# A diffusion trunk step on one core: first queries, unit copies, weight parts and memory masks take other places in the order of the work

## The chip, the cores and the metric

The kernel runs on one core of a Trainium2 chip. The metric is the time of one execution on the device, in microseconds (us); lower is better. Of several executions the median is given. A core has five engines that run side by side: PE (matmul; PEld is its weight load), DVE (vector), ACT (scalar and activation functions), POOL and SP; here SP and POOL issue the transfers between the chip's main memory and the core (DMA). Each engine works through its own queue in order; an instruction that must wait for another engine or a transfer holds up all that stand behind it in its queue.

## The reference

One layer of a trunk with 128 context tokens and 512 latent tokens (640 in all), width 1024: a gated feed-forward half step, a token mixer of two branches side by side, and a second half step. The two branches are what matters here:

```python
# differential attention, 8 heads, for a block of 128 queries
s = einsum('bqhcd,bkhcd->bhcqk', q, k) * scale          # two score maps (c = 0, 1)
pr = softmax(s)
w = pr[:, :, 0] - lam * pr[:, :, 1]
out = einsum('bhqk,bkhv->bqhv', w, v)
# mLSTM memory, 4 heads, two directions, over chunks of 128 tokens
b = cumsum(log_f); log_d = where(tril, b_t - b_s + i_s, -inf)
m_t = maximum(b + m, max(log_d)); dmat = exp(log_d - m_t)
s = (q k^T) * dmat
num = s v + exp(b + m - m_t) * (q C);  den = the same with n in place of C
h = num / maximum(abs(den), exp(-m_t))
C_new = decay * C + sum(w_s k_s v_s)
...
hm = rmsnorm(h_f + reverse(h_b)) * sigmoid(mo)
y = sigmoid(gm) * (hm @ w_br_m) + sigmoid(gd) * (att @ w_br_d)
```

Before the attention, queries and keys are normalised, and those of the latent tokens are rotated by their position (rope).

## The kernel before

All matmuls use float32 values in two parts: a high part that PE takes (`wH`, `hH`, `kH`, ...), made by a copy on ACT, and a low part (`wL`, `hL`, `kL`), the rest that remains, made by a subtraction on DVE. A product is then three matmuls (high x high, low x high, high x low). Helpers carry the lines that the profile shows: L51 is any ACT operation (`act`), L54 a DVE operation on two tensors (`tt`), L57 one with a scalar besides (`stt`), L61 one with a scalar alone (`ts`), L75 a matmul, L78 a transpose on PE. A scheduler places each engine's instructions; `written()` keeps what stands under it in the order of the code, and `issue_after(x)` keeps what stands under it behind instruction x.

**Projection units.** While the attention runs, a queue `fill` computes further projections in the gaps. `fill.units(n)` runs n units, each of 24 matmuls into a PSUM buffer `ps_t` (or `ps_p`), and a copy from it on ACT into `k_tok`, `q_tok`, `v_tok` or `stage`. `fill.ahead()` makes the high part `wH` of the next weights on ACT (128x2048, from the buffer `raw` that SP loads); `fill.low()` makes `wL` on DVE.

**Gate rows and the first head.** `gate_rows` turns the memory's gates into rows of numbers, step by step (`next(rows)`); its results are `fg`, `e`, `b`, `MP`, `dc`, `ig` on DVE, and ACT's exponentials of them, called `Q`. Around it stand head 0's keys (`kH`, `kL`), its queries (`queries()`, L1677: `qT` by a copy on ACT, then its low part by DVE at L54) and the first scores.

**Turns of the attention.** For each of 8 heads there are 5 turns of 128 queries: `scores` (PE, into `sc`), `soft` (DVE `mn`, ACT exponentials `p`, DVE `rc`, `r`, `p`), `mix` (PE transposes `ps_wT`, ACT copies `wT`), `values` of the turn before (PE, into `ps_o`). `aside` lets a step of the rotation (`rotate()`: `rope`, `rt`, `ry`, `qkt`, `qky`) run beside it. A table UNITS says how many units each turn has in its first and second part; n[1] is the second.

**The memory.** For each of 4 heads `load()` fetches `P` (rows of gate numbers, from `nm_dram`) and the values `va`, and adds the masks to both halves of `P` on DVE; `prep(i)` (i = 0 to 4) takes exponentials of `P` on ACT and multiplies by q k^T from `ps_st`. Then ten cells follow, numbered n = 0 to 9, each `cell()` with `ps_n` and `ps_u` on PE, `num` on ACT and DVE, `C` (the update) on DVE and `den` ending in a reciprocal (`at_vec`). A list `later[n]` holds what is issued behind cell n: the next head's `prep` behind cells 3 to 7, the last head's `finish` (`hs`, times `ry` and `g_mh`) behind cells 4 to 8. L814 is a DVE operation that computes modulation columns (`columns.tile`), placed between cells.

Of the kernel before, what the change touches and what calls it, by code (L numbers as in the profile page):

```python
# [7 lines left out]
F32 = mybir.dt.float32  # L8
# [3 lines left out]
ALU = mybir.AluOpType  # L12
# [19 lines left out]
def tile_trunk(ctx: ExitStack, tc: tile.TileContext, a: dict):  # L32
    nc = tc.nc
    vec = nc.vector
    as_written = [False]

    def placed(ins):
        if as_written[0] is in_row:
            i = ins.ins
            if i.engine in in_row:  # L40
                tc.add_manual_dep(
                    i, in_row[i.engine].name, mybir.DependencyInfo(mybir.DependencyClass.NoSync, mybir.DependencyReason.DATA),
                    reason="written",
                )
            in_row[i.engine] = i
        elif as_written[0]:
            tc.keep_in_program_order(ins)
        return ins

    def act(*args, **kw):  # L50
        return placed(nc.scalar.activation(*args, **kw))  # L51

    def tt(eng, out, in0, in1, op):
        return placed(eng.tensor_tensor(out=out, in0=in0, in1=in1, op=op))  # L54
# [13 lines left out]
    @contextmanager  # L68
    def written():
        was, as_written[0] = as_written[0], in_row  # L70
        yield
        as_written[0] = was
# [1335 lines left out]
    fill = Fill()  # L1408
# [94 lines left out]
    def gate_cols(j):  # L1503
        Q = Q_at[j]
        for i0, n in ((0, 4), (4, 1)):
            p = psum.tile([128, 4, 128], F32, tag="mm", name="ps_c")
            for i in range(n):
                tr(p[:, i, :], Q[:, (i0 + i) * 128 : (i0 + i + 1) * 128], ident)
            vec.tensor_copy(
                cols[:, i0 : i0 + n, 2 * j : 2 * j + 2, :].rearrange("p i q (d h) -> p i (q d) h", d=2),  # L1510
                p[:, :n].rearrange("p i (b c) -> p i b c", c=32)[:, :, :, 0:4],
            )
# [63 lines left out]
    def rotate():  # L1576

        if not rotations:
            return False
        first, second = rotations[0], rotations[1] if len(rotations) > 1 else []  # L1580
        had, left = len(first), len(second)
        with written():
            if had == 4 and left == 7 or had == 2 and left == 5:
                second.pop(0)()
            else:
                first.pop(0)()
                if (had, left) in ((5, 8), (4, 6)):
                    second.pop(0)()
            if not first:
                rotations.pop(0)  # L1590
        return True
# [53 lines left out]
    class Head:  # L1645
# [32 lines left out]
        def queries(self):  # L1678
            self.qT = ap.tile([128, 2, T], F32R, tag="qT", name="qT")
            self.ao = ap.tile([128, 5, 128], F32, tag="ao", name="ao")  # L1680
            self.at_q = act(self.qT, self.qd, AF.Copy)
            r = slice(64, 128)
            tt(vec, self.qT[r], self.qd[r], self.qT[r].bitcast(F32), ALU.subtract)

        def keys(self, *parts):
            if 0 in parts:
# [284 lines left out]
    heads = [Head(hd) for hd in range(8)]  # L1971
# [87 lines left out]
    rows = gate_rows(gt, ps_g)  # L2059
# [6 lines left out]
    with tc.issue_after(heads[0].at_copy.ins):  # L2066
        heads[0].keys(0, 1, 2)
    fill.units(1)
    next(rows)
    fill.units(2)  # L2070
    heads[0].queries()
    for _ in rows:
        pass
    fill.units(2)
# [2 lines left out]
    def aside(hd, qi, part):  # L2077
        if part == 0:
            with written():
                split = fill.low()  # L2080
            if qi < 4 and (UNITS[hd][qi][1] or not split):
                rotate()
        elif qi != 3:
            rotate()
        if (hd, part) == (0, 1) and qi < 2:
            gate_cols(qi)
# [6 lines left out]
    for hd in range(8):  # L2093
        H = heads[hd]
        odd = hd % 2
        N = heads[hd + 1] if hd < 7 else None
        for qi in range(5):
            n = UNITS[hd][qi]
            with written():
                H.scores(qi)  # L2100
                if qi > 0:
                    H.turn(qi - 1)
                if late is not None and qi == 2:
                    late()
                    late = None
                H.soft(qi)
            aside(hd, qi, 0)
            fill.units(n[0])
            with written():
                H.mix(qi)  # L2110
            if 0 < qi < 4 or hd == 7 and qi:
                with written():
                    H.values(qi - 1)
            if qi in (2, 3) and hd < 7:
                with written():
                    (N.turn_keys, N.turn_queries)[qi - 2]()
            if qi == 3 and hd < 7:
                N.load_cache()
            aside(hd, qi, 1)
            if (hd, qi) == (0, 2):  # L2120
                begin_pools()
            elif (hd, qi) == (6, 2):
                begin_memory()
            fill.units(n[1])
            if n[1]:
                rotate()
            with written():
                fill.ahead()
        n = UNITS[hd][-1]
        if hd < 7:  # L2130
            with written():
                fill.units(n[0])
                H.values(3)
                H.turn(4)
                N.keys(0)
                N.queries()
                N.keys(1, 2)
                fill.units(n[1])
                H.values(4)
            H.finish_norm()  # L2140
            with written():
                fill.ahead()
            fill.units(n[2])
            late = H.finish
        else:
            with written():
                H.turn(4)
            fill.eager = True
            fill.units(1)
            H.values(4)  # L2150
            H.finish_norm()
            fill.drain(3)
            with written():
                H.finish()
# [9 lines left out]
    mask = load(mp, [128, 2, 128], a["mask"], name="mask")  # L2164

    fill.pace(0.8, 1)
    class Memory:
# [6 lines left out]
        def load(self, fetch=nc.sync.dma_start):  # L2174
            h = self.h
            self.P = mp.tile([128, 5, 2, 128], F32, tag="P", name="P", bufs=2)
            self.va = mp.tile([128, 5, 258], F32, tag="va", name="va", bufs=2)
            for d in range(2):
                fetch(
                    out=self.P[:, :, d, :], in_=nm_dram[32 * d + h].partition_broadcast(128).rearrange("p (c t) -> p c t", c=5)  # L2180
                )
            fetch(out=self.va[:, :, 0:256], in_=v_dram[h])
            vec.memset(self.va[:, :, 256:257], 1.0)
            vec.memset(self.va[:, :, 257:258], 0.0)
            with ExitStack() as st:
              if h == 1:
                st.enter_context(tc.issue_after(mem[0].at_P.ins))
              for d in range(2):
                tt(vec, self.P[:, :, d, :], self.P[:, :, d, :], mask[:, d, None, :].to_broadcast([128, 5, 128]), ALU.add)
            self.ktok = mp.tile([128, 5, 256], F32, tag="ktok", name="mktok", bufs=2)  # L2190
            self.hs = mp.tile([128, 5, 256], F32, tag="hs", name="hs", bufs=2)

        def load_c(self):
            self.C = [load(mp, [128, 2, 258], a["c_aug"][d, self.h], tag=f"C{d}", name="C", bufs=2) for d in range(2)]
# [113 lines left out]
    mem = [Memory(h) for h in range(4)]  # L2308
    in_order[0] = True
    mem[0].load(dma)  # L2310
    mem[0].load_c()
    csil2 = ada_p.tile([128, 2, D], F32, name="csil")
    dma(csil2, csil_dram.partition_broadcast(128))
# [11 lines left out]
    for h in range(4):  # L2325
        m = mem[h]
        later = [[] for _ in range(10)]
        if h < 3:
            mem[h + 1].load()
            for i in range(5):  # L2330
                later[3 + i].append(lambda i=i: mem[h + 1].prep(i))
        if h > 0:
            for i in range(5):
                later[4 + i].append(lambda i=i: mem[h - 1].finish(i))
        if h == 3:
            for k in range(KT):
                later[2 + k].append(attended)
        later[9].append(m.gate)
        steps = [(s, 0, s >= 2, True, s < 3) if d == 0 else (3 - s, 1, s >= 2, True, s < 3) for s in range(4) for d in range(2)]
        steps += [(4, d, d == 1, False, True) for d in range(2)]  # L2340
        for n, (st, then) in enumerate(zip(steps, later)):
            if st[0] == 4 and st[1] == 0 and h < 3:
                mem[h + 1].load_c()
            m.cell(*st)
            if n in ((5,), (3, 7), (3, 7), ())[h]:
                columns.tile(m.at_vec)
            for f in then:
                f()
            fill.slot(0)
        m.stats()  # L2350
# [113 lines left out]
    for i in range(2):  # L2464
        r = raw[:, i * 1024 : (i + 1) * 1024]
# [7 lines left out]
    st = [Stats(x, hf, tmp) for hf in range(2)]  # L2473
# [224 lines left out]
```

## Time and profile before

| | us |
|---|---|
| median of 3 runs | 1796.81 |
| lowest and highest of them | 1793.94, 1798.72 |
| the profiled execution | 1796.18 |
| its span, from the first to the last instruction | 1794.3 |
| PE busy | 1767.4 (99%) |
| DVE busy | 1338.4 (75%) |
| ACT busy | 892.0 (50%) |

The span is the time between the first and the last instruction of the profiled execution; 1.88 us lie around it. A row of the timeline gives an instruction's start and duration in us, engine, line, operation, output<-inputs, shapes and a count; in brackets stand the engine's idle time before it and what ended that idle time.

### The profile page before, as it was taken

To read this page: it belongs to the slowest core of one execution; us is meant where nothing else is said; L and a number is where in the kernel's file an instruction comes from. 1 tells how busy PE (TensorE), PEld (TensorE's weight loads), DVE (VectorE), ACT (ScalarE), POOL (GpSimd) and SP (SyncE) were. 2 spreads that over 40 slices of the span, in tenths; PEclk is the share of its full clock that TensorE was granted. 3 is DMA by queue.
4 is the path that set the end of the run, shared out by engine and by line. 5 is a ranking of instruction groups with operands and counts; after the bars stand their busy time and mean duration, and the time that the engine had idled before them with its cause. 6 is when DMAs were issued, how large, how long until landed. Compare 5 with 4: busy or idle time off the path is not lost.

```text
span 1794.3 us, 29420 instructions
## 1 busy us (share of the span) xinstructions
PE 1767.4 (99%) x11790; PEld 1700.2 (95%) x11790; DVE 1338.4 (75%) x2136; ACT 892.0 (50%) x1563; POOL 40.8 (2%) x72
## 2 busy tenths in 40 slices
PE   8999999999999999999999999999999999999998
PEld 7999999999999999888889998899999999999998
DVE  5979897577889868776765637876768888896475
ACT  5554544332655555565655446562327545544432
POOL 0000000101000000000000000000000000000010
PEclk9999999999999999999999999999999999999999
DMA  8354565978235563333333345565642446557992
GB/s 321 121 200 159 197 243 197 368 224 279 92 109 197 180 188 88 107 105 102 105 119 126 126 157 167 205 235 200 219 165 77 152 160 197 205 176 276 354 311 84
DMA packets 149468, 327.03 MB, mean 182 GB/s; under 512 B 11537, under 2 KB 107537, under 8 KB 137553
## 3 DMA queue, kind: packets, MB, share of 16 engines
q1 hardware_dynamic: 137954, 279.38, 46.0%
q0 software_dynamic: 10688, 43.13, 7.4%
q10 hardware_dynamic: 688, 2.63, 0.4%
q8 instruction: 93, 1.52, 0.3%
q14 instruction: 45, 0.37, 0.1%
HBM read 243.12 MB, written 71.49 MB: 175 GB/s over the span
## 4 chain that ended last, share of the span: by engine, by line
PE 82%; DVE 8%; DMA 6%; ACT 3%; issue 1%; SPq 0%; DVEq 0%; ACTq 0%
PE ps_f L75 49%; PE ps_p L75 15%; PE ps_t L75 8%; PE sc L75 2%; PE ps_o L75 2%; DVE ww L54 2%; PE ps_n L75 1%; DMA P<-nm_dram 1%; DMA raw_a<-in_w_ada_k 1%; PE ps_wT L78 1%; DMA raw<-in_w2b 1%; DVE junk L814 1%; PE ps_u L75 1%; DMA a_raw<-aT_dram 1%; DVE wL L54 1%
## 5 line engine op out<-in xcount | busy, mean ns | idle before, releaser
L75 PE MATMUL ps_f<-S,ww 128*128 128x320 f32 x2400 | 387.0, 309 | 3.0 <-DMA S<-g_dram 1.0
L75 PEld LDWEIGHTS ps_f<-S,ww 128*128 128x128 f32 x2400 | 359.8, 188 | 7.0 <-DVE ww L54 4.6
L54 DVE TENSOR_TENSOR ww<-raw,ww 128x2048 fp32r<-128x2048 f32 (+1 forms) x73 | 163.9, 2245 | 65.3 <-ACT ww L51 65.2
L75 PE MATMUL ps_f<-hm,ww 128*128 128x320 f32 x1176 | 185.6, 309 | 0.1
L75 PEld LDWEIGHTS ps_f<-hm,ww 128*128 128x128 f32 x1176 | 175.7, 188 | 0.3 <-DVE ww L54 0.3
L51 ACT ACTIVATE ww<-raw 128x2048 fp32r<-128x2048 f32 (+1 forms) x73 | 136.8, 1874 | 56.6 <-DVE raw L54 32.8
L54 DVE TENSOR_TENSOR raw<-raw 128x1024 f32<-128x1024 f32 x186 | 160.9, 865 | 2.4
L75 PE MATMUL ps_f<-hm,wB 128*128 128x320 f32 x1008 | 161.5, 309 | 0.0
L75 PE MATMUL ps_p<-hH,wH 128*128 128x320 f32 x480 | 150.7, 314 | 2.1 <-DVE num L54 2.1
L75 PE MATMUL ps_t<-wH,hH 128*128 128x256 f32 (+1 forms) x440 | 150.8, 343 | 2.0 <-DVE x L57 0.9
L75 PEld LDWEIGHTS ps_f<-hm,wB 128*128 128x128 f32 x1008 | 151.3, 188 | 0.0
L75 PE MATMUL ps_p<-hH,wL 128*128 128x320 f32 x480 | 148.3, 309 | 0.0
L75 PE MATMUL ps_p<-hL,wH 128*128 128x320 f32 x480 | 148.3, 309 | 0.0
L75 PE MATMUL ps_t<-wH,hL 128*128 128x256 f32 (+1 forms) x440 | 146.4, 333 | 0.9 <-DVE hL L54 0.9
L75 PE MATMUL ps_t<-wL,hH 128*128 128x256 f32 (+1 forms) x440 | 146.2, 332 | 0.0
L51 ACT ACTIVATE u<-ps_f 128x320 f32<-128x320 f32 x129 | 55.7, 432 | 158.1 <-PE ps_f L75 157.9
L54 DVE TENSOR_TENSOR wL<-raw,wH 128x2048 fp32r<-128x2048 f32 x37 | 84.6, 2286 | 23.9 <-ACT wH L51 23.9
L51 ACT ACTIVATE wH<-raw 128x2048 fp32r<-128x2048 f32 (+1 forms) x45 | 75.4, 1681 | 48.4 <-PE ps_p L75 38.5
L54 DVE TENSOR_TENSOR wB<-raw,wB 128x1024 fp32r<-128x1024 f32 x64 | 78.1, 1220 | 24.1 <-ACT wB L51 24.1
L814 DVE CUSTOM_DVE_ANT_0 junk<-raw_a,csil 128x1024 bf16<-128x1024 f32 (+1 forms) x76 | 92.6, 1218 | 3.3 <-DMA raw_a<-in_w_ada_c 3.0
L75 PEld LDWEIGHTS ps_t<-wH,hH 128*128 128x128 f32 x440 | 83.8, 190 | 10.1 <-ACT nsq L51 1.1
L75 PEld LDWEIGHTS ps_p<-hH,wH 128*128 128x128 f32 x480 | 90.2, 188 | 3.0 <-DVE num L54 2.5
(305 smaller groups left out, 3526.2 us busy)
## 6 DMA issues: line engine op xcount, KB each, us to landing
g_dram<-g SPq DMA_DIRECT2D x44, 640.0 KB, 7.6
raw_a<-in_w_ada_c POOLq DMA_DIRECT2D x38, 512.0 KB, 5.1
g_dram<-g SPq DMA_DIRECT2D x24, 480.0 KB, 8.3
raw<-in_w1b SPq DMA_DIRECT2D x11, 1024.0 KB, 4.9
raw<-in_w3b SPq DMA_DIRECT2D x11, 1024.0 KB, 6.2
raw<-in_w1a SPq DMA_DIRECT2D x10, 1024.0 KB, 5.0
raw<-in_w3a SPq DMA_DIRECT2D x10, 1024.0 KB, 6.3
qk_d<-qk_t SPq DMA_DIRECT2D x64, 160.0 KB, 2.9
```

Source lines behind the costliest of these rows:

```text
L51: return placed(nc.scalar.activation(*args, **kw))
L54: return placed(eng.tensor_tensor(out=out, in0=in0, in1=in1, op=op))
L75: tc.keep_in_program_order(nc.tensor.matmul(*args, **kw))
L78: tc.keep_in_program_order(nc.tensor.transpose(*args, **kw))
L814: placed(vec.tensor_tensor_reduce(out=junk, in0=raw, in1=self.csil[:, v, :], op0=ALU.mult, op1=ALU.add, scale=1.0, scalar=0.0, accum_out=m ...
```

## The change

It has three parts. No arithmetic and no tile size is altered; PE's instructions stay as they are, in the same order.

1. Head 0's `queries()` are called ahead of the last two steps of `gate_rows`; the second of these is held behind the low part of `qT`.
2. In a turn, `fill.ahead()` moves. Where the turn's second part has units, it comes right behind them, in written order, and ahead of the further rotation step; where it has none, it comes ahead of the rotation step of `aside`.
3. The mask additions leave `load()` and become a function of their own, `masked()`. For head 0 it is called right behind the load, for heads 1 to 3 behind cell n = 2 of the head before, and held behind that cell's reciprocal.

```diff
-            tt(vec, self.qT[r], self.qd[r], self.qT[r].bitcast(F32), ALU.subtract)
+            self.at_low = tt(vec, self.qT[r], self.qd[r], self.qT[r].bitcast(F32), ALU.subtract)
...
     fill.units(1)
+    heads[0].queries()
     next(rows)
     fill.units(2)
-    heads[0].queries()
+    with tc.issue_after(heads[0].at_low.ins):
+        next(rows, None)
     for _ in rows:
         pass
...
+            if not n[1]:
+                with written():
+                    fill.ahead()
             aside(hd, qi, 1)
...
-            fill.units(n[1])
             if n[1]:
+                with written():
+                    fill.units(n[1])
+                    fill.ahead()
                 rotate()
-            with written():
-                fill.ahead()
...
-            with ExitStack() as st:
-              if h == 1:
-                st.enter_context(tc.issue_after(mem[0].at_P.ins))
-              for d in range(2):
-                tt(vec, self.P[:, :, d, :], self.P[:, :, d, :], mask[:, d, None, :].to_broadcast([128, 5, 128]), ALU.add)
...
+        def masked(self):
+            with ExitStack() as st:
+                if self.h:
+                    st.enter_context(tc.issue_after(mem[self.h - 1].at_vec.ins))
+                for d in range(2):
+                    P = self.P[:, :, d, :]
+                    tt(vec, P, P, mask[:, d, None, :].to_broadcast([128, 5, 128]), ALU.add)
...
     mem[0].load(dma)
+    mem[0].masked()
     mem[0].load_c()
...
             mem[h + 1].load()
+            later[2].append(mem[h + 1].masked)
```

What it does to the engines' queues shows at four places.

DVE ahead of the first scores, before (the rows from head 0's last keys to its first score maximum):

```order
L54 TENSOR_TENSOR kL<-qk_d,kH 128x2x128
L1472 COPY Ml<-lf 32x5
L61 TENSOR_SCALAR fg<-lf 64x640
L54 TENSOR_TENSOR wL<-raw,wH 128x2048
L54 TENSOR_TENSOR mn<-Ml,bl 64x5
L54 TENSOR_TENSOR e<-Q_6758,Ml 64x640
L54 TENSOR_TENSOR b<-fg,b 64x640
L54 TENSOR_TENSOR qT<-qk_d,qT 64x1280
```

The same place now:

```order
L54 TENSOR_TENSOR kL<-qk_d,kH 128x2x128
L54 TENSOR_TENSOR wL<-raw,wH 128x2048
L54 TENSOR_TENSOR qT<-qk_d,qT 64x1280
L1471 COPY Ml<-lf 32x5
L1472 COPY Ml<-lf 32x5
L1471 COPY bl<-b 32x5
L1472 COPY bl<-b 32x5
L1474 MEMSET MP 64x5
L61 TENSOR_SCALAR fg<-lf 64x640
L54 TENSOR_TENSOR e<-Q_6758,Ml 64x640
```

The low part of `qT` has moved ahead of `fg`, `e`, `mn` and `b`, and the copies `bl` and the clearing of `MP` have moved behind it from further up.

ACT in a turn with a unit in its second part, as one piece of the difference (the later of two such places, at 920 us, has `stage` where this one has `k_tok` and `q_tok`):

```order
-L51 ACTIVATE wH<-raw 128x2048
 L51 ACTIVATE rt<-rv 128x5
 L51 ACTIVATE k_tok<-ps_t 128x256
 L51 ACTIVATE q_tok<-ps_t 128x256
-L51 ACTIVATE wT<-ps_wT 128x512
-L51 ACTIVATE wT<-ps_wT 128x256
+L51 ACTIVATE wH<-raw 128x2048
 L51 ACTIVATE ry<-rt 128x5
```

The weight's high part now stands behind the copies out of PSUM and ahead of those of `wT`.

DVE in a turn without units, at 787 us (a second head has the same):

```order
 L54 TENSOR_TENSOR rt<-rt,rv 128x5
+L54 TENSOR_TENSOR wL<-raw,wH 128x2048
 L57 SCALAR_TENSOR_TENSOR ry<-rt,ry 128x5
+L1729 RECIPROCAL rc<-sm 128x2
 L54 TENSOR_TENSOR ao<-ao,ry 128x640
-L54 TENSOR_TENSOR wL<-raw,wH 128x2048
-L1729 RECIPROCAL rc<-sm 128x2
```

The low part moves ahead of `ry` and `ao`; nothing enters or leaves the stretch.

DVE in the first cells of memory head 1, before:

```order
L57 SCALAR_TENSOR_TENSOR C<-C,decay,ps_u 128x258
L54 TENSOR_TENSOR P<-P,mask 128x5x128
L54 TENSOR_TENSOR num<-ps_n_11326,num 128x258
L57 SCALAR_TENSOR_TENSOR C<-C,decay,ps_u 128x258
L61 TENSOR_SCALAR den<-num,cols 128x1
L54 TENSOR_TENSOR P<-P,mask 128x5x128
L57 SCALAR_TENSOR_TENSOR den<-num,den 128x1
```

In the same head now, two cells later:

```order
L57 SCALAR_TENSOR_TENSOR hs<-hs,ry,g_mh 128x256 x5
L57 SCALAR_TENSOR_TENSOR C<-C,decay,ps_u 128x258
L54 TENSOR_TENSOR num<-ps_n_11394,num 128x258
L57 SCALAR_TENSOR_TENSOR C<-C,decay,ps_u 128x258
L61 TENSOR_SCALAR den<-num,cols 128x1
L57 SCALAR_TENSOR_TENSOR den<-num,den 128x1
L2261 RECIPROCAL den<-den 128x1
L54 TENSOR_TENSOR P<-P,mask 128x5x128 x2
L57 SCALAR_TENSOR_TENSOR C<-C,decay,ps_u 128x258
```

The two masks, which before stood in the first cell, come behind cell 2's reciprocal, and all five `hs` of the head before now come ahead of cell 2's `C`.

ACT takes the exponentials of `P` with them. In head 1, before:

```order
L51 ACTIVATE P<-P,cols 128x128 x5
L51 ACTIVATE num<-ps_n_11350,cols 128x258
L51 ACTIVATE hjunk,hss<-hs 128x256
L51 ACTIVATE wv<-va,cols 128x258
L51 ACTIVATE P<-P,cols 128x128 x5
L51 ACTIVATE hs<-num,den 128x256
```

And now:

```order
L51 ACTIVATE wv<-va,cols 128x258
L51 ACTIVATE P<-P,cols 128x128 x3
L51 ACTIVATE mktok<-ps_k 128x256
L51 ACTIVATE P<-P,cols 128x128 x7
L51 ACTIVATE num<-ps_n_11456,cols 128x258
L51 ACTIVATE hs<-num,den 128x256
```

The ten exponentials stand closer together, with one copy between them, and the next cell's `num` stands behind all ten. On SP, the load of `raw` from `in_w_gd` goes ahead of the second load of `C`, and some loads and stores of the memory part change places.

## The prediction

> **What bounds the kernel now.** I read the page's busy times first, then PE's waits, then the timeline around each wait that the change can reach.
>
> ```profile
> PE 1767.4 (99%) x11790; PEld 1700.2 (95%) x11790; DVE 1338.4 (75%) x2136; ACT 892.0 (50%) x1563; POOL 40.8 (2%) x72
> 1100.00:1200.00 100.00, 96.07 (x554) 86.73 (x553) 80.09 (x257) 62.16 (x168) 0.00 (x0) 1.00 0.56 188
> ```
>
> The first row is the page's, the other is from a table by stretches of 100 us: after the times comes the busy time of PE, PEld, DVE, ACT and POOL, then PE's granted clock. PE is busy for 1767.4 of the span's 1794.3 us, so 26.9 us of idle is all that an edit can remove which leaves PE's own work as it is, and this one does: PE keeps its instructions and their order. The clock is full, so a longer or shorter run must come out of PE's waits. They are, with the total, the count and the longest:
>
> ```profile
> PE ps_p L75 <- DVE num L54: 2.1, 1, 2.1
> PE sc L75 <- DVE qT L54: 1.8, 1, 1.8
> PE ps_o L75 <- ACT wT L51: 1.3, 3, 0.5
> PE ps_u L75 <- DVE hs L57: 0.9, 1, 0.9
> PE sc L75 <- ACT p L51: 0.9, 2, 0.4
> PE ps_n L75 <- DVE C L57: 0.7, 1, 0.7
> PE ps_t L75 <- ACT q_tok L51: 0.6, 1, 0.6
> PE ps_t L75 <- ACT stage L51: 0.5, 1, 0.5
> ```
>
> These eight are 8.8 us, and they are what the change's places can touch; the other waits lie at the start, in the feed-forward parts, or where no order changes.
>
> **Part 1, the first queries.** PE reaches the first scores and waits for the low part of the queries, which DVE does last in a row of gate work.
>
> ```profile
> 679.90 0.28 PE L75 MATMUL ps_t<-wH,hL 128*128 128x256 f32 x1
> 682.02 0.50 PE L75 MATMUL sc<-kH,qT 128*128 128x512 f32 x1 [1.84 <-DVE qT L54]
> 675.59 0.41 DVE L54 TENSOR_TENSOR kL<-qk_d,kH 128x256 fp32r<-128x256 f32 x1
> 676.63 2.28 DVE L54 TENSOR_TENSOR wL<-raw,wH 128x2048 fp32r<-128x2048 f32 x1
> 680.48 1.49 DVE L54 TENSOR_TENSOR qT<-qk_d,qT 64x1280 fp32r<-64x1280 f32 x1
> 682.85 0.81 DVE L54 TENSOR_TENSOR ig<-fg,MP 64x640 f32<-64x640 f32 x1
> 683.76 0.72 ACT L51 ACTIVATE Q<-ig 64x640 f32<-64x640 f32 x1
> 684.38 0.36 ACT L51 ACTIVATE k_tok<-ps_t 128x256 f32<-128x256 f32 x1
> 686.87 0.36 PE L75 MATMUL ps_t<-wH,hH 128*128 128x256 f32 x1
> ```
>
> Now only kL and wL stand ahead of qT: 676.00 (kL's end) + 2.28 + 1.49 = 679.77. The 128x256 matmuls of this unit start every 0.12 us, as the ps_t row at 679.90 and its neighbours do, so PE is ready at 680.02, and its wait ends: 682.02 - 680.02 = 2.00 us (the idle column says 1.84, since it counts from the end of the last matmul). What is late next is the gate work. Before, it ran from kL's end at 676.00 to ig's end at 683.66, which is 7.66 us with wL's 2.28 and qT's 1.49 in it, thus 3.9 us of its own; two copies of bl, the clearing of MP and their kind also come behind qT now, for which I add 0.7. So ig ends near 679.77 + 4.6 = 684.4, 0.7 later than before. ACT's exponential of it (0.72) and then the k_tok copy (0.36) end near 685.5. That copy empties the buffer which the ps_t at 686.87 fills, and PE now comes there 2.00 earlier, at 684.87: a new wait of 0.6. Part 1 is worth 2.0 - 0.6 = 1.4 us, with ends at 0.8 (gate work as slow as 1.2 us behind) and 2.0 (none of it late).
>
> **Part 2, the order of a turn.** Where a turn has units of the projection, ACT now copies their result out of PSUM ahead of the weight's high part wH. At 830 and, in the same form, at 920 PE waited for that copy:
>
> ```profile
> 828.75 0.82 PE L78 MATMUL ps_wT<-ident,p 128*128 128x128 f32 x6
> 827.58 1.91 ACT L51 ACTIVATE wH<-raw 128x2048 fp32r<-128x2048 f32 x1
> 829.74 0.39 ACT L51 ACTIVATE q_tok<-ps_t 128x256 f32<-128x256 f32 x1
> 830.18 0.49 PE L75 MATMUL ps_t<-wH,hH 128*128 128x512 f32 x1 [0.62 <-ACT q_tok L51]
> 920.22 0.50 PE L75 MATMUL ps_t<-wH,hH 128*128 128x512 f32 x1 [0.53 <-ACT stage L51]
> ```
>
> Without the 1.91 us of wH ahead, the q_tok copy ends 1.9 earlier, at 828.2 + some tenths, and PE is ready at 829.57: both waits go. 0.62 + 0.53, and 0.16 more each as at the first scores, make 1.5 us. The wT copies and DVE's wL stand behind wH as before, some 1.2 us later at most, and their users come only after the unit's 24 matmuls. Ends: 0 (another copy holds PE) and 1.5.
>
> In turns without units wH now goes ahead of the rotation's steps. PE waits in two heads there, the first at 787:
>
> ```profile
> 787.32 1.60 PE L75 MATMUL ps_o<-v_tok,wT 128*128 128x128 f32 x12 [0.40 <-ACT wT L51]
> 789.36 0.50 PE L75 MATMUL sc<-kH,qT 128*128 128x512 f32 x1 [0.43 <-ACT p L51]
> 784.38 1.75 DVE L1715 TENSOR_REDUCE mn<-sc 128x2 f32<-128x1536 f32 x1
> 787.18 2.28 DVE L54 TENSOR_TENSOR wL<-raw,wH 128x2048 fp32r<-128x2048 f32 x1
> 789.83 1.02 DVE L57 SCALAR_TENSOR_TENSOR p<-p,r,p 128x768 f32<-128x768 f32 x1
> 790.91 0.88 PE L78 MATMUL ps_wT<-ident,p 128*128 128x128 f32 x6
> ```
>
> ACT gets free earlier and both waits can go, 0.83 a head or 1.15 with the 0.16s. But DVE works without a gap from 784.38 to p's end at 790.85, and PE takes that p at 790.91. The same instructions stand in that stretch after the change, wL only ahead of ry and ao. So PE arrives 1.15 earlier and waits 1.15 there. I take 0 for both heads, with 2.3 as the upper end and -0.5 as the lower.
>
> **Part 3, the memory's masks.** At the start of a memory head, DVE's next two mask additions stand in its queue until their data land, and work that PE needs stands behind them:
>
> ```profile
> 1083.34 0.82 DVE L54 TENSOR_TENSOR P<-P,mask 128x640 f32<-128x640 f32 x1 [2.29 <-DMA P<-nm_dram]
> 1084.61 1.14 PE L75 MATMUL ps_n<-C,mqT 128*128 128x258 f32 x4 [0.71 <-DVE C L57]
> 1102.12 0.83 DVE L54 TENSOR_TENSOR P<-P,mask 128x640 f32<-128x640 f32 x1 [2.56 <-DMA P<-nm_dram]
> 1103.33 0.41 PE L75 MATMUL ps_p<-hH,wH 128*128 128x320 f32 x1 [2.08 <-DVE num L54]
> 1108.90 0.48 DVE L57 SCALAR_TENSOR_TENSOR C<-C,decay,ps_u 128x258 f32<-128x258 f32 x1 [2.48 <-PE ps_u L75]
> 1137.33 0.67 PE L75 MATMUL ps_u<-wv,mktok 128*128 128x258 f32 x2 [0.88 <-DVE hs L57]
> ```
>
> Removed: 0.71 + 2.08 + 0.88 = 3.67, or 4.15 with 0.16 each. The instructions that take their place, by rows that group each kind:
>
> ```profile
> L54 DVE TENSOR_TENSOR P<-P,mask 128x640 f32<-128x640 f32 x8 | 6.6, 822 | 9.6 <-DMA P<-nm_dram 9.6
> L51 ACT ACTIVATE P<-P,cols 128x128 f32<-128x128 f32 x40 | 12.6, 392 | 8.4 <-DVE P L54 8.3
> L57 DVE SCALAR_TENSOR_TENSOR hs<-hs,ry,g_mh 128x256 f32<-128x256 f32 x20 | 8.4, 479 | 0.0
> L814 DVE CUSTOM_DVE_ANT_0 junk<-raw_a,csil 128x1024 bf16<-128x1024 f32 (+1 forms) x76 | 92.6, 1218 | 3.3 <-DMA raw_a<-in_w_ada_c 3.0
> ```
>
> Per head that is two masks, 6.6/8 x 2 = 1.65 us of DVE, and ten exponentials, 12.6/40 x 10 = 3.15 us of ACT, now both in the middle of the cells. In head 0 (1084) the next C update still stands behind the masks and only one cell later: I count +0.5 of 0.87. In head 1 the five hs rows (8.4/20 x 5 = 2.1 us) come before cell 2's C. The C at 1108.90 has 2.48 us of room for them, but PE arrives 2.2 earlier now, so the room is spent; then come the masks (1.65) and one L814 (1.22) ahead of the C's of cells 3 and 4, where 2.1 of hs stood: 2.87 - 2.1 = 0.8 more. I count 2.24 - 2.2 = 0. In head 2 the hs rows again come before the C that PE takes next: 1.04 - 1.1 = -0.1. On SP one raw load of 1 MB goes ahead of the second C load, which the next head needs only in its first cell; some loads swap with stores. I cost these at nothing under the cells that lie between; if that cover is gone, a late landing shows as PE waiting for C. Sum: +0.4, with ends at +4.15 and, if cells must also wait for half of the ten exponentials in three heads, 4.15 - 3 x (1.65 + 1.6) = -5.6.
>
> **Sum.** 1.4 + 1.5 + 0 + 0.4 = 3.3 us less. The profiled execution took 1796.18 (span 1794.3 and 1.88 around it), 0.63 under the median of the runs, 1796.81. The median becomes 1793.5. A measurement of this kernel tells about 0.3%, 5.4 us, from no change, so this would read as the same.
>
> **The rivals.** (a) All removed waits stay removed: 2.0 + 1.5 + 2.3 + 4.15 = 9.95 less, 1786.9. For it speaks that DVE is 75% and ACT 50% busy; against it the full DVE stretch at 784 to 791. (b) Waits only move: part 1's gate work, the DVE chain at 787 and the cells take back all but some tenths, 1796.5. For it: PE is the bound and the other two run just ahead of it at each of these places. (c) The masks' new place costs more than it saves, one mechanism: ACT does its ten exponentials in a row, and the next cell's num copy, which frees PE's ps_n buffer, stands behind them. At -5.6 for part 3 the sum is 1.4 + 1.5 - 5.6 = -2.7 and the time 1799.5. It is slower than before from 2.9 us of net new waits on, about 1 us a head. Against it: num of one cell is needed only when PE comes round to the buffer, and none of the eight waits above is for num by ACT, though the ten exponentials already stood in these cells as two fives. [...]
>
> [...]
>
> **How the numbers follow.** Forecast 0.52, (a) 0.20, (b) 0.18, (c) 0.08, (d) 0.02. Time 1793.5. The forecast's own range is 1790.5 to 1796 (its parts' uncertain halves). The whole range goes from 1788.0, near (a), to 1798.0, past (b); (c), (d) and half of (a) are left out. Faster by over 0.3% (under 1791.4): (a) and a little of the forecast, 0.24. Slower by over 0.3% (above 1802.2): half of (d) and a part of (c), 0.05. Same: 0.71.
>
> **What would show it.** Right: no wait of sc for qT, a ps_t wait of about 0.6 for k_tok some 5 us behind; none for q_tok or stage; ps_wT waiting about 1.1 for p in two heads; no ps_p wait for num, but new ps_n or ps_u waits for C of about 1 us each in heads 1 and 2. Wrong would be: ps_wT without a wait (then 2.3 more is gained), ps_n or ps_u waits of over 2 us a head, ACT's wH of in_w_gd landing late so that ps_p waits for it, or a clock below 1.00.

## The result, and the profile after

The changed kernel takes 1790.3 us (median of 6 runs, 1788.69 to 1790.93), the kernel before 1796.66 (median of 6, 1793.81 to 1798.72). The ratio is 0.9965 with a 95% interval from 0.9952 to 0.9978: 6.4 us less. A second series beside the experiments gave 1789.72 against 1797.25, ratio 0.9954 (0.9939 to 0.9968). So the change is worth 0.35 to 0.46%, about twice the forecast 3.3 us. In the experiments below, one of the 12 executions with part 2 alone took 2896.25 us at a granted clock of 0.556, and all ratios are taken without it.

From the page and from two tables by stretches, after:

```profile
PE 1769.2 (99%) x11790; PEld 1702.8 (95%) x11790; DVE 1338.1 (75%) x2136; ACT 892.2 (50%) x1563; POOL 40.8 (2%) x72
1100.00:1200.00 100.00, 98.07 (x574) 89.44 (x573) 80.96 (x252) 66.02 (x169) 0.00 (x0) 1.00 0.57 199
12.00:30.00 18.00, 17.34 (x138) 13.03 (x142) 8.99 (x23) 6.42 (x12) 0.00 (x0) 0.81 1.03 405
```

The same instructions run in a span of 1788.8 us (1790.56 for the whole execution), and PE's idle time falls from 26.9 to 19.6 us. The third row is a trap for whoever compares two profiles: in this execution PE's clock was 0.81 early on, in work that the change does not touch (1.00 in the same stretch of the profile before), and PE reached the attention 2.1 us later than in the profile before. The whole spans therefore understate the gain, and from here on I compare the start of the same matmul in two traces and look for the places where the offset between them steps.

PE's waits after, those in the parts that the change reaches:

```profile
PE ps_wT L78 <- DVE p L57: 2.3, 3, 0.8
PE ps_n L75 <- DVE C L57: 1.2, 1, 1.2
PE ps_u L75 <- DVE C L57: 0.6, 1, 0.6
PE ps_o L75 <- ACT wT L51: 0.5, 1, 0.5
```

Of the eight rows shown before, qT, num, hs, p at sc, q_tok and stage are gone; wT is down from 1.3 to 0.5 and p at ps_wT is up from 0.7 to 2.3. The steps, in us (minus is sooner):

| place | forecast | changed kernel | with that part alone |
|---|---|---|---|
| first scores, then k_tok behind them | -2.0, +0.6 | -2.01, +0.32 | -2.01, +0.28 |
| unit copies at 830 and 920 | -1.5 | -0.86, -0.77 | -0.86, -0.77 |
| turns without units, two heads | 0 | -0.43 | -0.47 |
| memory head 0 | -0.5 | -0.87 | -0.88 |
| memory head 1 | 0 | -2.44, +0.77, +1.34 | -2.44, +0.55, +1.35 |
| memory head 2, first cells | +0.1 | -1.04, +0.29, +0.19 | -1.04, +0.19 |
| later in the memory (1156, 1167) | not counted | -0.54, -0.75 | -0.54, -0.76 |

They add up to -6.8 in the changed kernel. From the first scores to the memory's end the offset moves by 7.5 in all; of the rest 0.24 lies at the scores at 743 us, and each part alone shows about as much there, so it is the gain of none of them. The rows behind the new waits, from the timeline:

```profile
790.78 0.87 PE L78 MATMUL ps_wT<-ident,p 128*128 128x128 f32 x6 [0.81 <-DVE p L57]
879.70 0.55 PE L78 MATMUL ps_wT<-ident,p 128*128 128x128 f32 x3 [0.83 <-DVE p L57]
1106.88 1.54 DVE L54 TENSOR_TENSOR P<-P,mask 128x640 f32<-128x640 f32 x2
1108.87 0.70 PE L75 MATMUL ps_u<-wv,mktok 128*128 128x258 f32 x2 [0.61 <-DVE C L57]
1109.97 1.21 DVE L814 CUSTOM_DVE_ANT_0 raw_a<-raw_a,csil 128x1024 bf16<-128x1024 f32 x1
1111.00 0.46 ACT L51 ACTIVATE num<-ps_n,cols 128x258 f32<-128x258 f32 x1
1111.64 0.70 PE L75 MATMUL ps_n<-va,P 128*128 128x258 f32 x2 [1.18 <-DVE C L57]
```

The first answers to 790.91 before, where PE took p without a wait, and the second is the same place in the other head. The others are head 1: the masks, and then an L814, stand just ahead of a C for which PE waits.

### The profile page after: what moved, and what is told of

It reads as the page before. It is cut to its first block, busy times and chain, and to the rows that moved or that the text cites. A ratio compares the mean times of both kernels' runs of the same rounds, so it can differ in the third digit from the quotient of the medians.

```text
span 1788.8 us, 29433 instructions
## 1 busy us (share of the span) xinstructions
PE 1769.2 (99%) x11790; PEld 1702.8 (95%) x11790; DVE 1338.1 (75%) x2136; ACT 892.2 (50%) x1563; POOL 40.8 (2%) x72
## 4 chain that ended last, share of the span: by engine, by line
PE 85%; DVE 8%; DMA 3%; ACT 2%; issue 1%; SPq 0%; DVEq 0%; ACTq 0%
PE ps_f L75 49%; PE ps_p L75 15%; PE ps_t L75 9%; PE ps_o L75 2%; PE sc L75 2%; PE ps_n L75 2%; DVE ww L54 2%; PE ps_wT L78 1%; PE ps_u L75 1%; DVE wL L54 1%; DMA raw<-in_w2b 1%; DVE junk L814 1%; DMA out_new_c<-Cn 1%; DMA raw<-in_w2a 1%; DMA raw_a<-in_w_ada_k 1%
## 5 line engine op out<-in xcount | busy, mean ns | idle before, releaser
L814 DVE CUSTOM_DVE_ANT_0 junk<-raw_a,csil 128x1024 bf16<-128x1024 f32 (+1 forms) x76 | 92.5, 1217 | 2.9 <-DMA raw_a<-in_w_ada_c 2.7
L75 PEld LDWEIGHTS ps_t<-wH,hL 128*128 128x128 f32 x440 | 83.5, 190 | 9.9 <-DVE hL L54 1.1
```

The source lines that it names most:

```text
L75: tc.keep_in_program_order(nc.tensor.matmul(*args, **kw))
L814: placed(vec.tensor_tensor_reduce(out=junk, in0=raw, in1=self.csil[:, v, :], op0=ALU.mult, op1=ALU.add, scale=1.0, scalar=0.0, accum_out=m ...
```

## The experiments

### The three parts alone

Each part of the change was put on the kernel before by itself. Part 1:

```diff
     fill.units(1)
+    heads[0].queries()
     next(rows)
     fill.units(2)
-    heads[0].queries()
+    with tc.issue_after(heads[0].at_low.ins):
+        next(rows, None)
```

> Only part 1 (head 0's queries ahead of the last gate rows) on the kernel before. Local theory (each part's gain is made at its own place and the three add up): PE reaches the first scores without the wait for qT, 2.0 us earlier than before, gives back 0.3 at the ps_t some 5 us later, so 1.7 us less in all; every later wait as before (ps_o and sc at 787 and 877, ps_t at 830 and 920, the memory's five). Rival (a wait only moves): the waits at 787 or 830 grow by what part 1 gains, and the time is within 0.5 us of before.

Measured: 1794.58 against 1796.21, ratio 0.9992 (0.9983 to 1.0001): by the ratio 1.4 us less, with an interval that just takes in none. The steps are -2.01 and +0.28 at the forecast place, and the attention's later waits stay. That is the local theory, though the time alone would not settle it. In the memory, where it expected no change, three waits step by -0.87, -0.56 and +0.52.

Part 2:

```diff
+            if not n[1]:
+                with written():
+                    fill.ahead()
             aside(hd, qi, 1)
...
-            fill.units(n[1])
             if n[1]:
+                with written():
+                    fill.units(n[1])
+                    fill.ahead()
                 rotate()
-            with written():
-                fill.ahead()
```

> Only part 2 (unit copies ahead of wH, wH ahead of rotation steps) on the kernel before. Local theory: the two ps_t waits for q_tok and stage go (0.62 and 0.53 in the idle column, about 1.6 us by PE's starts), the ps_o and sc waits go in both heads (1.15 each) and a ps_wT wait for p of about 0.8 comes in each, so some 0.2 net each: 2.1 us less in all; the wait for qT (1.84) stays. Rival (moved only): the ps_wT waits take back all of 1.15 and the unit copies' gain returns in the next turn: under 1 us.

Measured: 1794.0 (the median of all 12), ratio 0.9986 (0.9977 to 0.9995): by the ratio 2.5 us less. Both unit copies' waits are gone, and in each of the two heads -0.56 and -0.6 are followed by +0.93, so 0.2 is left. By the starts this is 2.1 in all, as expected, and refutes the rival's "under 1 us"; the interval of the time, 0.9 to 4.1, does not quite.

Part 3:

```diff
             mem[h + 1].load()
+            later[2].append(mem[h + 1].masked)
```

(with `masked()` in place of the additions in `load()`).

> Only part 3 (memory masks behind cell 2 of the head before) on the kernel before. Local theory: the memory's waits as in the changed kernel: none for C in head 0, none for num at ps_p, a ps_u wait for C of 0.6 and a ps_n wait for C of 1.2 in head 1, and the two waits of before at 1156 (ps_st for num, 0.4) and 1167 (ps_n for Cn, 0.6) gone too; 3.3 us less in all. Rival (those two late waits went because PE came earlier from parts 1 and 2, or because of chance in the transfers): they stay, and the time falls by 2.0 or less.

Measured: 1793.51, ratio 0.9985 (0.9976 to 0.9995): 2.7 us less, and nearly every memory step of the changed kernel is there. The two late waits went. The one at 1167 stays at 0.59 with part 1 alone and with part 2 alone, so it belongs to part 3, not to an earlier PE. The one at 1156 is less clear: it is 0.29 with part 1 alone, and gone with part 2 alone. Parts 2 and 3 alone each bring a wait of 0.5 for ACT's `mkT` near 1070 and 1076, which the changed kernel does not have.

The savings of the three parts are 0.08, 0.14 and 0.15%, together 0.37%, beside 0.35 and 0.46% for the whole: within their intervals of about 0.1 each, the parts add up. How close the sum comes is in part luck, since in this kernel an execution's time goes with its granted clock. Of the kernel before, beside these runs, 11 executions at 1.000 have a median of 1795.55, 9 at 0.999 of 1796.37, and 7 at 0.998 of 1798.04. Among those at 1.000 alone the parts are worth 1.4, 3.6 and 3.2 us (6, 6 and 3 executions), 8.2 together, and the changed kernel in its second series 6.8 (4 against 5).

One step cannot be booked to part 3, though. With part 1 alone the masks still stand in their old place, and yet head 0's wait for C was gone too. DVE's masks in that run (the first answers to 1083.34 before, which waited 2.29; the second to 1102.12, which waited 2.56):

```profile
1081.44 0.82 DVE L54 TENSOR_TENSOR P<-P,mask 128x640 f32<-128x640 f32 x1 [1.24 <-DMA P<-nm_dram]
1099.66 0.82 DVE L54 TENSOR_TENSOR P<-P,mask 128x640 f32<-128x640 f32 x1 [2.00 <-DMA P<-nm_dram]
```

The rows of P came about 1 us sooner there relative to DVE, and with part 2 alone likewise. So head 0's 0.87 looks like the luck of a transfer in one profiled execution, but the kernel before was profiled only once, and this is not shown.

### Why the late waits went

The two waits at 1156 and 1167 are on ACT's `num` and `Cn`, which stand behind copies of `a_raw`. ACT before, then after, and then the load's two issues before, with part 1 alone, after, and with part 3 alone (last column: us from issue to landing):

```profile
1154.35 1.99 ACT L51 ACTIVATE aHL<-a_raw 128x640 fp32r<-128x640 f32 x3 [1.75 <-DMA a_raw<-aT_dram]
1156.75 0.49 PE L75 MATMUL ps_st<-mqT,mkT 128*128 128x128 f32 x2 [0.38 <-ACT num L51]
```

```profile
1149.05 1.99 ACT L51 ACTIVATE aHL<-a_raw 128x640 fp32r<-128x640 f32 x3 [0.20 <-DMA a_raw<-aT_dram]
```

```profile
a_raw<-aT_dram SPq DMA_DIRECT2D x2, 960.0 KB, 5.9
a_raw<-aT_dram SPq DMA_DIRECT2D x2, 960.0 KB, 6.0
a_raw<-aT_dram SPq DMA_DIRECT2D x2, 960.0 KB, 4.7
a_raw<-aT_dram SPq DMA_DIRECT2D x2, 960.0 KB, 4.8
```

With the masks in the new place the load lands 1.2 us sooner after its issue, and ACT hardly waits for it. In those two kernels SP issues the load of `g_mh`, which stood right ahead of `a_raw` before, early: at 1135.89 in the changed kernel instead of 1147.46, since the `hs` rows that free its buffer now come early in head 2. (With part 2 alone, in the old order, the median is 5.6.) That this is what makes the landing faster was not tried by itself.

### What holds PE in memory head 1

```diff
-            if n in ((5,), (3, 7), (3, 7), ())[h]:
+            if n in ((5,), (5, 7), (3, 7), ())[h]:
                 columns.tile(m.at_vec)
```

> The changed kernel with the first modulation column of memory head 1 behind cell 5 in place of cell 3, so that no L814 stands ahead of cell 4's C update on DVE. Theory DVE: the 1.2 us ps_n wait for C at 1111 is L814's 1.21 us, it goes, and 1.2 us less than the changed kernel is seen there by PE's starts. Rival ACT: the ten exponentials in a row hold num until 1111.0, and PE then waits for num in place of C: under 0.4 us less there. Either way a later place may pay for the moved L814 (the low weight part then stands behind more of DVE's work: up to 1 us).

Measured: 1789.84, ratio 0.9968 (0.9956 to 0.9980), not told apart from the changed kernel. In head 1 the +0.77 and +1.34 shrink to +0.20: the DVE theory holds for this order. But a later place takes more than the forecast 1 us: ACT now stands idle for 3.88 us ahead of `Cn`, until the store lands that frees its buffer, and PE waits for it:

```profile
1132.41 0.66 ACT L51 ACTIVATE Cn<-ps_u 128x258 f32<-128x258 f32 x2 [3.88 <-DMA out_new_c<-Cn]
1132.85 0.70 PE L75 MATMUL ps_u<-wv,mktok 128*128 128x258 f32 x2 [2.22 <-ACT Cn L51]
1135.00:1136.00 1.00, 1.00 (x4) 0.74 (x3) 1.00 (x7) 0.89 (x3) 0.00 (x0) 0.50 1.02 341
```

The first row is ACT, the second PE, the third the table by stretches: behind that wait PE's clock is at 0.50, and the matmuls start 0.43 us apart where it was 0.22. So against the changed kernel 1.9 us gained are paid back as 2.4 of wait and about 1.5 of slow clock. The profiled execution, 1791.88, is one of the two longer ones of five (the others are 1789.1 to 1789.84). In it the store was issued at 1124.26, behind the loads of `P` and `va`, and ACT went on at 1132.41; in the changed kernel it was issued ahead of them at 1124.62, and ACT went on at 1128.19. So again the order of SP's transfers has changed; that this is the cause was not tried.

With L814 behind cell 0 instead, `(0, 7)`:

> The changed kernel with head 1's first modulation column (L814) behind cell 0 in place of cell 3, where DVE has some idle time, and not behind cell 5, where the later weight part and a store's wait paid for it. Theory DVE: the 1.2 us ps_n wait for C in head 1 goes without a later place paying, 1.0 to 1.9 us less than the changed kernel by PE's starts from 1076 to 1140. Rival (PE is just ahead of DVE and ACT throughout the cells, so a wait removed there comes back within the head): less than 0.5 us less.

Measured: 1791.38, ratio 0.9967 (0.9957 to 0.9977), and here the rival is right. Head 1's two waits for C are gone (-0.77 and -1.34), and PE waits in the same cells for `num`, which ACT reaches behind its ten exponentials; a wait of 0.41 for C comes in head 2:

```profile
1107.72 0.44 PE L78 MATMUL ps_k<-ident,mkT 128*128 128x128 f32 x2 [0.58 <-ACT num L51]
1110.61 0.44 PE L78 MATMUL ps_hT<-ident,hs 128*128 128x128 f32 x2 [1.50 <-ACT num L51]
```

With the masks behind cell 1 in place of cell 2, `later[1].append(mem[h + 1].masked)`:

> The changed kernel with the masks behind cell 1 of the head before in place of cell 2. Theory (the place of the masks is what counts): in head 0 DVE is back at the masks before their rows have landed, so a PE wait for C of 0.7 to 0.9 returns near 1082; in head 1 the masks no longer stand between cells 2 and 3, so the 0.6 wait of ps_u goes, but masks and the five hs rows (1.6 + 2.1 us) now both stand ahead of cell 2's C, where PE waits about 1 us: 0.5 to 1.5 us more than the changed kernel. Rival (place does not matter, only that the masks left the start of the head): within 0.3 us of it.

Measured: 1791.06, ratio 0.9969 (0.9959 to 0.9980), 0.8 above the changed kernel's first series, though the intervals overlap. Head 0's wait for C did not come back, even though DVE stood there for the rows:

```profile
1078.89 0.83 DVE L54 TENSOR_TENSOR P<-P,mask 128x640 f32<-128x640 f32 x1 [1.63 <-DMA P<-nm_dram]
```

PE reached its matmul only as the C behind these masks ended, and waited 0.05. Head 1's two waits are gone, by -0.77 and -1.34; in their place come +0.57 and +0.41 ahead of them, for ACT's `mkT` and `num`, and +0.44 and +1.20 later in the head. The time is where it was expected, but cannot tell the two theories apart; the places are others. The three variants say the same: in head 1 DVE, ACT and PE are all busy for most of the time (of the 8 us from 1104, in the run with L814 behind cell 5, for 7.76, 6.69 and 7.96), and what is taken off one wait appears at a later one.

### The chain behind ps_wT

The softmax's `rc`, `r`, `p` of the second turn are written ahead of wL:

```diff
                 H.soft(qi)
+                if qi == 1 and not n[1]:
+                    H.mix(qi)
             aside(hd, qi, 0)
             fill.units(n[0])
-            with written():
-                H.mix(qi)
+            if qi != 1 or n[1]:
+                with written():
+                    H.mix(qi)
```

> The changed kernel with the low weight part wL behind the softmax's p in the second turn of each head (rc, r, p are written ahead of it). Theory DVE chain: at 787 and 877 PE now waits 0.81 for p because wL's 2.28 us stand ahead of it; that wait goes, about 0.93 by PE's starts in each of two heads and a part of the third ps_wT wait, so 1.9 us less than the changed kernel. Rival ACT: p waits for the exponentials, which end where wL did, and the wait stays; or the next unit waits for the late wL: under 0.5 us less, or up to 1 us more.

Measured: 1789.45, ratio 0.9961 (0.9947 to 0.9974), not told apart from the changed kernel. At 790 and 879 the starts step by -0.98 each: wL did stand in the way of p. Some 17 us later in the same heads they step back:

```profile
806.20 0.39 PE L75 MATMUL sc<-kH,qT 128*128 128x256 f32 x1 [0.37 <-ACT p L51]
807.81 0.85 PE L78 MATMUL ps_wT<-ident,p 128*128 128x128 f32 x6 [0.87 <-DVE p L57]
```

PE, a microsecond sooner, meets the next p, two turns on. Neither theory had this place.

### How long a wait may last

In the run of part 3 alone the first scores waited as before, but what followed did not look as before:

```profile
683.39 0.62 PE L75 MATMUL sc<-kH,qT 128*128 128x512 f32 x1 [2.00 <-DVE qT L54]
684.00:685.00 1.00, 1.00 (x6) 0.90 (x5) 1.00 (x3) 0.74 (x1) 0.00 (x0) 0.50 0.92 267
686.00:687.00 1.00, 1.00 (x6) 1.00 (x5) 0.82 (x1) 0.11 (x1) 0.00 (x0) 0.50 0.04 3
```

The clock is 0.50 for 3.4 us behind a wait of 2.00. To see the price, the changed kernel was given such a wait again, by two, then by four repeats of one subtraction with the same values:

```diff
+            with written():
+                for _ in range(2 if self.hd == 0 else 0):
+                    tt(vec, self.kL[:, :, 0:512], self.kd[:, :, 0:NS], self.kH[:, :, 0:512].bitcast(F32), ALU.subtract)
+                self.at_low = tt(vec, self.qT[r], self.qd[r], self.qT[r].bitcast(F32), ALU.subtract)
```

Two theories were set against each other: that a wait of 2 us can be followed by half a clock, as the 2.00 was with part 3 alone, and that a wait of that length leaves the clock at 1.00, as 1.84 and 2.08 did in the kernel before.

> The changed kernel with two needless repeats of a kL subtraction (1.23 us each, same values) ahead of the first queries' low part, so that PE waits about 2.1 us again at the first scores. Theory clock: a wait of 2 us can be followed by some 3 us at half the granted clock, as in the run with part 3 alone (wait 2.00, then 0.50) and not in the kernel before (wait 1.84, then 1.00); here it is seen in the profile, or in some of the timed runs as 1 to 1.5 us more than the wait itself explains: 2.1 to 3.6 us more than the changed kernel. [...]

> As the run with two repeats, with four: PE waits about 4.5 us at the first scores. Both theories expect the clock at one half behind it for some 3 us; by PE's starts 4.5 us of wait and 1.5 of slower matmuls, 6 us more than the changed kernel. If the clock stays at 1.00, neither holds and the time is 4.5 us more.

Measured: 1792.47 and 1794.3, ratios 0.9976 (0.9967 to 0.9985) and 0.9988 (0.9979 to 0.9997). The waits were shorter than meant, since DVE had more room than I had counted:

```profile
681.19 0.50 PE L75 MATMUL sc<-kH,qT 128*128 128x512 f32 x1 [1.33 <-DVE qT L54]
```

```profile
683.85 0.50 PE L75 MATMUL sc<-kH,qT 128*128 128x512 f32 x1 [3.95 <-DVE qT L54]
685.00:686.00 1.00, 1.00 (x5) 0.81 (x5) 1.00 (x4) 0.01 (x1) 0.00 (x0) 0.50 0.09 25
```

The first row is of the run with two repeats, the others of that with four. Behind 1.33 the clock stays at 1.00, behind 3.95 it falls to 0.50. The first run cannot tell its two theories apart, as it never waited 2 us. By the starts of the same matmuls, from 423 us to the memory's end, the second run falls 5.8 us behind the changed kernel, near the 6 expected; the medians differ by less (4.0 to 4.6), as start-ups differ. None of its 10 executions has a granted clock of 1.000 over the whole (4 of 10 with two repeats), which fits a half clock in each of them, and not in the profile alone. The first falls 3.0 behind by the memory's end, 1.5 of it the wait and 0.6 a wait for p at the next scores; what makes up the rest stays open.

The changed kernel was timed once more beside these:

> The changed kernel once more, timed beside the kernel before and the variants on one chip: 0.9965 of the kernel before (5.3 to 7.4 us less), and its runs closer together than those of the kernel before, since its longest waits of about 2 us, which can be followed by a slower clock, are gone from the attention and the memory.

Measured: 1789.72, ratio 0.9954 (0.9939 to 0.9968), lowest and highest 1787.67 and 1792.27 (the kernel before 1795.23 to 1801.79 beside it). Four of its 5 executions have a clock of 1.000, and 5 of the 16 before; that is too few to call the runs closer together. No variant beats the changed kernel by more than its spread.

## Why the prediction was right or wrong

The time lies in the whole range (1788.0 to 1798.0), if 0.2 below the forecast's own (1790.5 to 1796), and the direction is right. The size is not: 6.4 us where 3.3 was forecast, and 0.35% is just past the line of 0.3% that I gave a chance of 0.24. By the steps of the working:

**Part 1, right.** -2.01 for the wait (forecast 2.00), as read from PE's spacing and not from the idle column. The new delay behind the k_tok copy came at the very instruction named, at 0.3 instead of 0.6. By the starts part 1 alone is worth 1.7. That its time came out at 1.4, the number forecast, says little, with an interval from -0.2 to 3.1.

**Part 2, units: right.** -1.63 against -1.5; no other copy held PE.

**Part 2, turns without units: the mechanism right, the size a little off.** Both waits went, PE waits for p instead, 0.81 and 0.83, but 1.15 was not taken back whole: -0.43 in all instead of 0. The step that failed is "the same instructions stand in that stretch, wL only ahead of ry and ao": they do, but in this order they take less time. From mn to the end of p it was 784.38 to 790.85, 6.47 us, and it is now 784.58 to 790.73, 6.15 us:

```profile
784.58 1.75 DVE L1715 TENSOR_REDUCE mn<-sc 128x2 f32<-128x1536 f32 x1
788.52 0.16 DVE L57 SCALAR_TENSOR_TENSOR ry<-rt,ry 128x5 f32<-128x5 f32 x1
788.60 0.16 DVE L1729 RECIPROCAL rc<-sm 128x2 f32<-128x2 f32 x1
789.71 1.02 DVE L57 SCALAR_TENSOR_TENSOR p<-p,r,p 128x768 f32<-128x768 f32 x1
```

Before, `ry`, `ao` and `r` each stood right behind the step whose result they take, and started about 0.2 us after it:

```profile
786.05 0.16 DVE L54 TENSOR_TENSOR rt<-rt,rv 128x5 f32<-128x5 f32 x1
786.24 0.17 DVE L57 SCALAR_TENSOR_TENSOR ry<-rt,ry 128x5 f32<-128x5 f32 x1
786.44 0.82 DVE L54 TENSOR_TENSOR ao<-ao,ry 128x640 f32<-128x640 f32 x1
789.39 0.16 DVE L1729 RECIPROCAL rc<-sm 128x2 f32<-128x2 f32 x1
789.58 0.22 DVE L57 SCALAR_TENSOR_TENSOR r<-sm,nlam,rc 128x1 f32<-128x1 f32 x1
```

Now a step that does not need the one ahead stands in between and follows at once (`rc` 0.08 us behind `ry`, and wL 0.07 behind `rt`). That this makes up the whole 0.3 us is read from the rows, not tried by itself.

**Part 3: under-sized, by 2.3 us in the timed run (-2.7, 0.9 to 4.3, against -0.4).** Head 1 was as forecast: what was removed came back at the masks and the L814, -0.33 net. The slips lie elsewhere. In head 2 I put the hs rows against the wait for them and got -0.1; PE then lost only 0.48 of the 1.04. The largest is a sentence at the start: I set aside all waits "where no order changes", among them the two at 1156 and 1167, because the masks have no part in them. Their 1.29 went with part 3, where a load lands 1.2 us sooner (0.54 of it, at 1156, went with part 2 alone as well). I had costed the order of SP's loads at nothing, and looked only for a loss there. Head 0's 0.87 cannot be booked to part 3, as the runs of parts 1 and 2 show. Of the signs named, the new waits for C of about 1 us each came in head 1 (0.61 and 1.18) and hardly in head 2 (0.12).

**The rivals.** (a) asked that all removed waits stay removed; they did not, at ps_wT and in head 1. (b) is refuted by the time itself, and by the starts in the three parts, which each keep more than half of what they remove. (c) did not come about in the sum: the ten exponentials hold `num` only when something else does not hold PE first (1.50 in the run with L814 behind cell 0). (d), a slower clock behind long waits, did not come about: from 19.98 us to 1788 the changed kernel's clock was 1.00. What the forecast charged for it was my estimate, and no run shows it. The runs showed 0.50 for about 3.4 us behind waits of 2.00, 2.22 and 3.95, which cost about 1.5 us behind the 2.22, and 1.00 behind waits of 2.08 and 2.18.

## What to carry to other kernels

Where PE is 99% busy and its order is fixed, list every wait and ask of each whether the engine that ends it gets free or only has its work turned round: in this kernel the first kind paid, and the second moved the wait further on. Include the waits that hang on a transfer, even those far from the edit, since moving work on DVE moves when buffers come free and so when loads are issued (here that of `g_mh`, at 1135.89 instead of 1147.46). And before a difference of 2 us between two profiles is explained, compare starts of the same matmul: start-up and single transfers differ by that much between executions of one kernel (the changed kernel's two profiles, 1788.8 and 1786.7 us long, are 1.8 us apart at the same matmul at 423 us).

## What the runs showed of the hardware

PE's clock fell to 0.50 for about 3.4 us behind waits of 2.00 (part 3 alone), 2.22 (L814 behind cell 5) and 3.95 us (four repeats). In the profile of the changed kernel it was 0.50 for 6.83 us, from 13.15 to 19.98, behind a wait of 2.26 in the start-up, which is the 0.81 of the first table. With L814 behind cell 0, three waits of 0.58, 0.23 and 1.50 us came within 3.5 us; of the matmuls behind them the four of `ps_n` with C took 1.91 us, where such a four took 1.03 at 1126.98 with L814 behind cell 5, and the clock of that execution was 0.999 over the whole. The clock stayed at 1.00 behind 1.33 (two repeats) and behind 1.84 and 2.08 (the kernel before), and also behind 2.18, at the first scores with part 2 alone, in an execution whose clock was 1.000 over the whole:

```profile
681.59 0.50 PE L75 MATMUL sc<-kH,qT 128*128 128x512 f32 x1 [2.18 <-DVE qT L54]
```

So the length of the wait alone does not decide; what else does was not shown.

Where the clock falls, a long wait is dearer than its row: in the run with L814 behind cell 5, about 1.5 us on top of 2.22.
